# One hybrid encoder layer on one core: weight sums of the last stage in additions of 512 columns, with a new instruction order

## The chip, the cores and the metric

The kernel runs on one NeuronCore of one Trainium2 chip. The metric is device time in microseconds (us) of one execution, as a median over several. The core's engines, by the names that the profile uses, are PE (TensorE, matmuls; PEld is its weight load), DVE (VectorE), ACT (ScalarE), POOL (GpSimd) and SP (SyncE, which here only issues DMAs; SPq in the timeline). Each engine works through its own instructions in the order in which the program emits them, and waits where an operand or a room in memory is not yet there.

## The reference, cut to what matters

One layer for a prompt of 1024 tokens and a sample group of 32 tokens with 512 cached positions; the weights are shared, everything is float32.

```python
def in_proj(h, g_pre, w_in):
    u = rmsnorm(h, g_pre) @ w_in            # (.., 1024) @ (1024, 4096)
    qa, ka, va, ga, qb, kb, vb, gb = jnp.split(u, SPLIT_IDX, axis=-1)   # 8 x 512
...
def band_attention(q, k, v, q_pos, k_pos, bias_table):   # 8 heads of 64, chunks of 64
    s = jnp.einsum('bqhd,bkhd->bhqk', q, k) * ATTN_SCALE + bias_table[:, rel][None]
    ok = (k_pos >= 0) & (kc <= qc) & (kc >= qc - N_PREV_CHUNKS)
    w = jax.nn.softmax(jnp.where(ok, s, NEG_INF), axis=-1)
    return jnp.einsum('bhqk,bkhd->bqhd', w, v)

def stick_breaking(q, k, v, q_pos, k_pos):               # 8 heads of 64
    log_beta = jax.nn.log_sigmoid(z)
    log_1m = jnp.where(causal, jax.nn.log_sigmoid(-z), 0.0)
    after = lax.cumsum(log_1m, axis=3, reverse=True) - log_1m
    w = jnp.where(causal, jnp.exp(log_beta + after), 0.0)
    return jnp.einsum('bhqk,bkhd->bqhd', w, v)
...
def finish(h, oa, ga, ob, gb, w_out, g_post, p, w_ple, w_ple_gate):
    y = jnp.concatenate([oa * jax.nn.silu(ga), ob * jax.nn.silu(gb)], axis=-1) @ w_out
    h = h + rmsnorm(y, g_post)
    return h + jax.nn.sigmoid(h @ w_ple_gate) * (p @ w_ple)
```

## The kernel before

**Precision.** A float32 product is made of three matmuls of a fast format: each operand is split into a high part (h) and a low part (l), and h·h, h·l and l·h are summed in PSUM. For a weight, a DMA brings the raw tile (`wr`), ACT casts the high part (`wh`), POOL subtracts for the low part (`wl`). For attention weights the same is called `wTh` (ACT) and `wTl` (DVE).

**Stages.** After the norm of the input, the eight projections qA, kA, vA, gA, qB, kB, vB, gB are computed for one pair of heads at a time (`mm_kA2` in the program is k of group A, pair 2). Prompt and sample go through them together, 1056 tokens as three chunks of 352 columns. The heads follow in stages 1 to 8, two in each: A0, B0, A1, B1, A2, B2, A3, B3. In a stage with heads A1, for instance, PE alternates between the scores and products of attention and the projections that the next stage needs. Stages 3, 4, 7 and 8 also hold a share of the sample's attention (tiles with s in the name: `SsB0`, `PVsA0`).

**A head.** A head has eight blocks of 128 queries. The scores (`SA`, `SB`) go through DVE, ACT and POOL as tiles `be`. Then the weights must be transposed: for the first blocks PE does that (`ptwA`, `ptwB`), for the last three of A (5, 6, 7) and blocks 4 to 6 of B the tile is stored to memory (`swapA11_7` is block 7 of head 1 of pair A1), read back by four DMAs and transposed by DVE. ACT and DVE split it, and PE multiplies it with v: `PVA`, `PVB`, once for blocks 0 to 3 and once for blocks 4 to 7.

**The weight sums.** The last stages (9 to 13) multiply by w_out ("o") and w_ple_gate ("g") with a seven-product Strassen-Winograd scheme, for which sums T1 to T4 of quarters of the weights are needed. They are made ahead of time in the attention stages: stages 1 and 2 for "o", 5 and 6 for "g". `sum_weights` (L1703) loads four blocks of 128x512 (`oB…`, `gB…`; the tag `sg` has three rooms), has POOL add or subtract four times and stores each result (`sum_dro`, `sum_drg`) for the last stage to load. Eight calls make 32 sums. Each sum is two POOL instructions of 256 columns now (L1708 to L1712).

**What sets the order.** The program does not run as written. A Recorder notes every operation with its dependencies (so all rows of the profile name line L781, in the changed kernel L772, and are told apart by tile names). `order()` (L549) then plans: a forward simulation with costs for each operation, and after it `PASSES` times a backward pass that gives each operation a due time and another forward simulation by due time. In the last one the due time of an operation is shifted by a number from two tables, `AHEAD_OF` (by engine and kind of tile) and `AHEAD_AT` (by stage, engine and kind; L28 to L97). The planner lets a POOL operation and a DVE operation that reads two operands from SBUF not run at the same time (`shared`). The rooms of tiles and PSUM banks are dealt in the planned order too. All DMAs go out from SP, in one line.

**Rooms that matter here.** Raw weights `wr` have four rooms, which tiles of the sample's attention use too: `wr_kA2` must wait for the last matmul of `PVsA0`, and `wr_vA2` for the last of `SsB0`; so do the weights of gA0 for `PVsA1`.

Of the kernel before, what the change touches and what calls it, by code (L numbers as in the profile page):

```python
# [28 lines left out]
    ('ACT', ''): -307, ('ACT', 'L'): -414, ('ACT', 'Qfs'): -110, ('ACT', 'Qhs'): -859,  # L29
    ('ACT', 'S'): -381, ('ACT', 'be'): 32, ('ACT', 'g'): 244, ('ACT', 'gT'): -473,  # L30
    ('ACT', 'hnh'): 1092, ('ACT', 'kd'): 363, ('ACT', 'newh'): -483, ('ACT', 'o'): -50,
    ('ACT', 'om'): -5, ('ACT', 'p'): -1128, ('ACT', 'sq'): 108, ('ACT', 'stk'): 127,
    ('ACT', 'stq'): -682, ('ACT', 'wh'): -79, ('ACT', 'whS'): -249, ('ACT', 'xS'): -955,
    ('ACT', 'xb'): -149, ('ACT', 'yb'): -199, ('DVE', ''): -1363, ('DVE', 'Kl'): 290,
# [7 lines left out]
    ('PE', 'ptxs'): 7, ('POOL', 'be'): 315, ('POOL', 'bias'): 960, ('POOL', 'g'): 573,  # L42
    ('POOL', 'ksS'): 1098, ('POOL', 'om'): -712, ('POOL', 'r'): -536, ('POOL', 'sgg'): 1213,
# [5 lines left out]
}  # L49
AHEAD_AT = {  # L50
    (0, 'ACT', 'hnh'): -902, (0, 'ACT', 'pleo'): 783, (0, 'ACT', 'sq'): 26, (0, 'ACT', 'v'): -215,
    (0, 'PE', 'mm'): -297, (0, 'PE', 'ple'): 252, (0, 'POOL', 'wl'): -634, (0, 'SP', 'wpr'): 528,
    (0, 'SP', 'wr'): -232, (0, 'SP', 'x'): -74, (1, 'ACT', 'ot'): -442, (1, 'ACT', 'wTh'): 589,
    (1, 'ACT', 'wh'): 43, (1, 'DVE', 'S'): 928, (1, 'DVE', 'om'): 258, (1, 'DVE', 'wTl'): 279,
    (1, 'PE', 'S'): -86, (1, 'SP', 'sum'): -1097, (2, 'ACT', 'L'): 674, (2, 'ACT', 'be'): -112,
    (2, 'ACT', 'ot'): -548, (2, 'ACT', 'vt'): 555, (2, 'ACT', 'wTh'): 152, (2, 'DVE', 'om'): 60,
    (2, 'DVE', 'vt'): 389, (2, 'PE', 'S'): 43, (2, 'SP', 'o'): 677, (2, 'SP', 'sum'): 621,
    (3, 'ACT', 'Qfs'): 130, (3, 'ACT', 'stq'): 1238, (3, 'ACT', 'wh'): 323, (3, 'DVE', 'L'): -248,
    (3, 'DVE', 'Vh'): 390, (3, 'DVE', 'Vl'): 233, (3, 'DVE', 'diags'): 564, (3, 'DVE', 'om'): 40,
    (3, 'DVE', 'ot'): 169, (3, 'DVE', 'over'): 620, (3, 'DVE', 'vt'): 997, (3, 'DVE', 'vx'): 1005,  # L60
# [3 lines left out]
    (4, 'ACT', 'stq'): 92, (4, 'ACT', 'wTh'): -49, (4, 'DVE', 'Kl'): 168, (4, 'DVE', 'S'): 37,  # L64
    (4, 'DVE', 'Vl'): 530, (4, 'DVE', 'newl'): -393, (4, 'DVE', 'om'): -78, (4, 'DVE', 'v'): 323,
# [3 lines left out]
    (5, 'ACT', 'stv'): 620, (5, 'ACT', 'wTh'): 828, (5, 'ACT', 'wh'): 111, (5, 'DVE', 'S'): 706,  # L69
# [13 lines left out]
    (8, 'ACT', 'om'): -708, (8, 'ACT', 'ot'): -106, (8, 'ACT', 'sgg'): -442, (8, 'ACT', 'wTh'): 312,  # L83
    (8, 'DVE', 'Kcs'): -163, (8, 'DVE', 'Kl'): 236, (8, 'DVE', 'S'): 304, (8, 'DVE', 'Vl'): 1322,
# [702 lines left out]
def stream_step(  # L787
# [7 lines left out]
    nc = rec  # L795
# [1481 lines left out]
```

## Time and profile before

| | us |
|---|---|
| three executions | 766.77, 769.12, 770.49 (median 769.12) |
| the profiled execution | 767.52 |
| its span, first to last instruction | 765.7 |
| PE busy in the span | 755.8 |
| granted clock of PE | 1.000 of full speed |

The span is what the profile shows; the execution's own time is 1.8 us longer. The profile's rows read as follows: in the timeline, start and duration in us, engine, line, operation, the tile written and the tiles read (numbers at the end of names left out), their shapes and how many instructions the row joins; in brackets the idle time of the engine before it and what ended it. In the waits, total idle time, number of times and the longest. In the stretches, for PE, PEld, DVE, ACT and POOL in this order the busy time, with the number of instructions in brackets.

### The profile page before, as it was taken

How to read it: one execution, taken by the hardware profiler on the slowest of the kernel's cores; microseconds unless marked ns; L12 is line 12 of the kernel's file. 1: busy time of each engine (PE TensorE's matmuls, PEld its weight loads, DVE VectorE, ACT ScalarE, POOL GpSimd, SP SyncE). 2: the span in 40 equal slices, each digit the busy share in tenths (PEclk: the TensorE clock that was granted, in tenths of full speed). 3: DMA queues.
4: the chain of work that ended last, by engine and by line, in shares of the span. 5: the costliest groups of instructions: out<-in, count | busy, mean ns of one | idle time of the engine just before them, and what ended most of it. 6: DMA issues, size and time to landing. Idle time of an engine off the chain costs nothing.

```text
span 765.7 us, 14211 instructions
## 1 busy us (share of the span) xinstructions
PE 755.8 (99%) x4410; PEld 699.5 (91%) x4410; DVE 615.7 (80%) x1067; ACT 525.1 (69%) x1122; POOL 447.7 (58%) x503
## 2 busy tenths in 40 slices
PE   9999999999999999999999999999999999999997
PEld 7999999999998999999999999999998877888786
DVE  7837878898879999989798898887455688988985
ACT  6647767787766768876977786764337877784561
POOL 5623626953257555566772566778552449698453
PEclk9999999999999999999999999999999999999999
DMA  8748888778878849988878889995798856868846
GB/s 305 238 132 208 240 192 261 211 198 232 218 194 233 226 119 241 257 247 254 228 195 250 219 215 229 247 271 159 240 288 271 264 185 203 325 180 256 296 144 204
DMA packets 202525, 173.73 MB, mean 227 GB/s; under 512 B 67009, under 2 KB 164649, under 8 KB 202450
## 3 DMA queue, kind: packets, MB, share of 16 engines
q1 hardware_dynamic: 202450, 172.83, 78.7%
q8 instruction: 35, 0.57, 0.3%
q14 instruction: 40, 0.33, 0.1%
HBM read 105.72 MB, written 58.91 MB: 215 GB/s over the span
## 4 chain that ended last, share of the span: by engine, by line
PE 86%; DMA 5%; DVE 3%; ACT 2%; issue 1%; SPq 1%; POOL 0%; ACTq 0%; DVEq 0%; POOLq 0%
PE mm_vA L781 6%; PE mm_kB L781 6%; PE mm_qA L781 6%; PE mm_gA L781 6%; PE mm_gB L781 6%; PE mm_kA L781 6%; PE mm_qB L781 5%; PE PVB L781 4%; PE SA L781 3%; PE ple L781 3%; PE SB L781 3%; PE PVA L781 3%; PE o3P L781 3%; PE o1P L781 3%; PE g1P L781 3%; PE g0P L781 3%
## 5 line engine op out<-in xcount | busy, mean ns | idle before, releaser
L781 POOL TENSOR_TENSOR be<-be 128x256 f32<-128x256 f32 (+8 forms) x66 | 84.7, 1290 | 47.6 <-ACT be L781 17.8
L781 DVE TENSOR_TENSOR_SCAN be<-be,SB 128x384 f32<-128x384 f32 (+5 forms) x96 | 91.8, 962 | 12.0 <-ACT be L781 5.6
L781 ACT ACTIVATE be<-SB 128x384 f32<-128x384 f32 (+5 forms) x192 | 85.2, 499 | 18.2 <-DVE be L781 9.1
L781 DVE TENSOR_TENSOR wTl<-be,wTh 128x640 fp32r<-128x640 f32 (+2 forms) x48 | 58.6, 1228 | 4.5 <-ACT wTh L781 3.6
L781 DVE STREAM_TRANSPOSE be<-be 128x640 f32<-128x640 f32 (+3 forms) x56 | 47.7, 865 | 5.4 <-DMA be<-in_cache_b_k_dram 2.7
L781 ACT ACTIVATE be<-be,statA 128x640 f32<-128x640 f32 (+3 forms) x64 | 44.4, 695 | 10.2 <-DVE statA L781 10.0
L781 ACT CAST wTh<-be 128x640 fp32r<-128x640 f32 (+2 forms) x48 | 37.5, 785 | 4.3 <-DMA be<-swapB 2.9
L781 POOL TENSOR_TENSOR gB<-gB,gB 128x256 f32<-128x256 f32 x32 | 26.4, 845 | 18.5 <-DMA gB<-in_w_ple_gate_dram 18.5
L781 POOL TENSOR_TENSOR oB<-oB,oB 128x256 f32<-128x256 f32 x32 | 26.3, 837 | 12.7 <-DMA oB<-in_w_out_dram 10.7
L781 PE MATMUL SB<-kdB,LB 128*128 128x384 f32 (+5 forms) x96 | 33.0, 348 | 0.0
L781 PE MATMUL SB<-klB,LB 128*128 128x384 f32 (+5 forms) x96 | 33.0, 345 | 0.0
L781 DVE CUSTOM_DVE_ANT_0 be<-SA,biasA 128x320 f32<-128x320 f32 (+2 forms) x64 | 29.4, 481 | 4.0 <-PE SA L781 3.1
L781 PE MATMUL SA<-kdA,LA 128*128 128x320 f32 (+2 forms) x96 | 30.5, 322 | 0.0
L781 PE MATMUL SA<-klA,LA 128*128 128x320 f32 (+2 forms) x96 | 30.1, 317 | 0.0
L781 ACT CAST wTh<-ptwB 128x512 fp32r<-128x512 f32 (+3 forms) x48 | 22.4, 485 | 10.2 <-PE PVB L781 5.6
L781 DVE TENSOR_TENSOR wTl<-ptwB,wTh 128x512 fp32r<-128x512 f32 (+3 forms) x48 | 25.2, 543 | 3.8 <-ACT wTh L781 3.6
L781 PE MATMUL ptwB<-ident,be 128*128 128x128 f32 x144 | 26.7, 273 | 1.1 <-DVE be L781 0.7
L781 POOL TENSOR_TENSOR klA<-stkA,kdA 64x1024 fp32r<-64x1024 f32 (+2 forms) x9 | 19.9, 2215 | 10.9 <-ACT kdA L781 10.8
L781 DVE TENSOR_TENSOR LA<-stqA,LA 64x1024 fp32r<-64x1024 f32 (+2 forms) x9 | 16.7, 1857 | 10.4 <-ACT LA L781 10.2
L781 DVE TENSOR_TENSOR wTl<-ptwA,wTh 128x128 fp32r<-128x128 f32 (+3 forms) x48 | 22.1, 480 | 3.6 <-ACT wTh L781 3.4
L781 POOL TENSOR_TENSOR h<-h,x 128x512 f32<-128x512 f32 (+1 forms) x18 | 23.4, 1320 | 1.3 <-DVE h L781 1.3
L781 PE MATMUL PVB<-wTh,v2B 128*128 128x512 f32 (+1 forms) x96 | 24.1, 344 | 0.0
(694 smaller groups left out, 2652.3 us busy)
## 6 DMA issues: line engine op xcount, KB each, us to landing
swapA<-be SPq DMA_DIRECT2D x24, 320.0 KB, 3.8
be<-swapA SPq DMA_DIRECT2D x96, 80.0 KB, 2.5
oB<-in_w_out_dram SPq DMA_DIRECT2D x16, 256.0 KB, 4.5
sum_dro<-oB SPq DMA_DIRECT2D x16, 256.0 KB, 3.2
gB<-in_w_ple_gate_dram SPq DMA_DIRECT2D x16, 256.0 KB, 4.3
sum_drg<-gB SPq DMA_DIRECT2D x16, 256.0 KB, 3.3
x<-in_x_prompt_dram SPq DMA_DIRECT2D x16, 256.0 KB, 4.5
h_dr<-h SPq DMA_DIRECT2D x8, 512.0 KB, 4.5
```

The source lines that it names most:

```text
L781: getattr(getattr(tc.nc, o.what[0]), o.what[1])(*args, **kw)
```

## The change

The loop over two slices in `sub` becomes one instruction; the planner runs 2 passes in place of 9; and both tables of shifts are other tables altogether.

```diff
 AHEAD_OF = {
-    ('ACT', ''): -307, ('ACT', 'L'): -414, ('ACT', 'Qfs'): -110, ('ACT', 'Qhs'): -859,
...
+    ('ACT', 'Kh'): 207, ('ACT', 'L'): -556, ('ACT', 'be'): 73, ('ACT', 'g'): 1388,
...
 BANKS = {'mm': 1, 'S': 2, 'T': 1, 'PV': 1}
-PASSES = 9
+PASSES = 2
 PE_LATEST = True
...
         def sub(out, x, y, op):
             rec.low = 1
-            for c in (slice(0, 256), slice(256, 512)):
-                nc.gpsimd.tensor_tensor(out[:, c], x[:, c], y[:, c], op)
+            nc.gpsimd.tensor_tensor(out, x, y, op)
             rec.low = 0
```

PE, ACT, DVE and SP have the same operations as before, in another order (4410, 1021, 1067 and 918 recorded operations); POOL has 471 in place of 503.

Three places show what moved. The first is SP's queue at the weights of kA2, where heads A1 end and B1 begin (`wr_kA` raw weights, `be<-in_cache_b_k_dram` reads of the sample's cache, `o_dr<-diagsA` small stores, `be<-swapA` reads of a score tile for its transposition). Before:

```order
L781 DMA oB_2904<-in_w_out_dram 128x512
L781 DMA be<-in_cache_b_k_dram 32x16x32 x3
L781 DMA wr_kA_0_3032<-in_w_in_dram 128x4x128
L781 DMA be<-in_cache_b_k_dram 32x16x32
L781 DMA wr_kA_1_3033<-in_w_in_dram 128x4x128
L781 DMA wr_qA_0_3035<-in_w_in_dram 128x4x128
L781 DMA o_dr_63<-diagsA_2919 32x2x32 x2
L781 DMA o_dr_64<-diagsA_2919 32x2x32 x2
L781 DMA be<-swapA_7_133 32x4x160 x4
L781 DMA be<-in_cache_b_k_dram 32x16x32
L781 DMA wr_qA_1_3036<-in_w_in_dram 128x4x128
```

With the change:

```order
L772 DMA be<-swapA_7_133 32x4x160
L772 DMA wr_kA_0_3002<-in_w_in_dram 128x4x128
L772 DMA wr_kA_1_3003<-in_w_in_dram 128x4x128
L772 DMA o_dr_63<-diagsA_2854 32x2x32 x2
L772 DMA o_dr_64<-diagsA_2854 32x2x32 x2
L772 DMA be<-swapA_7_133 32x4x160 x3
L772 DMA o_dr_64<-otA_0_0_3024 64x256
L772 DMA o_dr_64<-otA_0_1_3045 64x256
L772 DMA wr_qA_0_3009<-in_w_in_dram 128x4x128
L772 DMA wr_qA_1_3010<-in_w_in_dram 128x4x128
L772 DMA be<-in_cache_b_k_dram 32x16x32 x8
```

The cache reads, four of which stood among the weights, and the load of a w_out block now follow behind them all.

The second is SP's queue at the weights of vA2, in the stage of heads B1 (`sum_dro<-oB` stores a weight sum, `vnsB` is the sample's v). Before:

```order
L781 DMA ks_drA<-ktA_3258 128x32
L781 DMA sum_dro<-oB_3358 128x512
L781 DMA vnsB_3557<-vs_drB 32x4x32
L781 DMA wr_vA_0_3565<-in_w_in_dram 128x4x128
L781 DMA vnsB_3557<-vs_drB 32x4x32
L781 DMA wr_vA_1_3580<-in_w_in_dram 128x4x128
```

With the change:

```order
L772 DMA vnsB_3502<-vs_drB 32x4x32 x2
L772 DMA wr_vA_0_3524<-in_w_in_dram 128x4x128
L772 DMA wr_vA_1_3545<-in_w_in_dram 128x4x128
L772 DMA o_dr_68<-otB_1_0_3554 64x256
L772 DMA o_dr_68<-otB_1_1_3559 64x256
```

The store of a sum has left the place ahead of the weights, and their two halves stand together.

The third is POOL at head B20, where it makes products over the score tiles (`be<-be`) block by block, wider from block to block, and weight sums between them. Before:

```order
L781 TENSOR_TENSOR be<-be 128x128
L781 TENSOR_TENSOR gB_4478<-gB_4478,gB_4469 128x256
L781 TENSOR_TENSOR be<-be 128x256
L781 TENSOR_TENSOR be<-be 128x384
L781 TENSOR_TENSOR be<-be 128x512
L781 MEMSET be 128x1
L781 TENSOR_TENSOR gB_4478<-gB_4478,gB_4469 128x256
L781 TENSOR_TENSOR gB_4469<-gB_4469,gB_4487 128x256
L781 TENSOR_TENSOR be<-be 128x640
```

With the change:

```order
L772 TENSOR_TENSOR be<-be 128x128
L772 TENSOR_TENSOR gB_4467<-gB_4467,gB_4417 128x512
L772 TENSOR_TENSOR be<-be 128x256
L772 TENSOR_TENSOR be<-be 128x384
L772 TENSOR_TENSOR be<-be 128x512
L772 MEMSET be 128x1
L772 TENSOR_TENSOR be<-be 128x640
L772 TENSOR_TENSOR be<-be 128x768
```

The first sum is whole ahead of the 256-column product, and the second pair of halves, which stood ahead of the 640-column product, is gone from there; the other sums follow later. In SP's queue at head A31 the store of a sum (`sum_drg<-gB`) moves from behind the reads of blocks 6 and 7 to ahead of them, and the cache reads from among them to behind.

More of the change, by code (lines that the diff above doesn't have):

```diff
@@ L28 @@
 AHEAD_OF = {
-    ('ACT', ''): -307, ('ACT', 'L'): -414, ('ACT', 'Qfs'): -110, ('ACT', 'Qhs'): -859,
[L30 to L34, printed above, removed]
@@ new lines @@
+    ('ACT', 'junk'): -1269, ('ACT', 'kd'): -317, ('ACT', 'newh'): 105, ('ACT', 'oT'): 655,
+    ('ACT', 'oj'): 829, ('ACT', 'ot'): 82, ('ACT', 'p'): -600, ('ACT', 'sg'): -246,
+    ('ACT', 'sq'): 1488, ('ACT', 'stk'): 373, ('ACT', 'stv'): 281, ('ACT', 'v'): 135,
+    ('ACT', 'vt'): -245, ('ACT', 'wTh'): -31, ('ACT', 'wh'): 193, ('ACT', 'whS'): -371,
+    ('ACT', 'whs'): -848, ('ACT', 'x'): 202, ('ACT', 'xS'): 146, ('DVE', 'Kcs'): -377,
+    ('DVE', 'S'): -118, ('DVE', 'Vh'): -1234, ('DVE', 'cc'): 663, ('DVE', 'diags'): -443,
@@ new lines @@
+    ('DVE', 'gj'): -557, ('DVE', 'h'): -248, ('DVE', 'lg'): -1145, ('DVE', 'lo'): 399,
+    ('DVE', 'newl'): -1399, ('DVE', 'o'): 417, ('DVE', 'ot'): -206, ('DVE', 'over'): 261,
+    ('DVE', 'sgg'): 69, ('DVE', 'sq'): -1331, ('DVE', 'ug'): -293, ('DVE', 'vx'): -746,
+    ('DVE', 'w'): -563, ('DVE', 'wl'): 252, ('DVE', 'wlS'): -338, ('DVE', 'wph'): 67,
+    ('PE', 'PVs'): -129, ('PE', 'Ss'): 57, ('PE', 'g'): -716, ('PE', 'mm'): -8,
+    ('PE', 'ptws'): 69, ('PE', 'ptx'): -592, ('PE', 'ptxs'): 19, ('POOL', 'be'): -148,
@@ L49 @@
+    ('POOL', 'gT'): -366, ('POOL', 'ogg'): 1173, ('POOL', 'om'): -1329, ('POOL', 'r'): 738,
[4 rows of a table added]
 }
 AHEAD_AT = {
[L51 to L60, printed above, removed]
[3 rows of a table removed]
@@ L77 @@
-    (7, 'ACT', 'be'): 447, (7, 'ACT', 'kd'): -699, (7, 'ACT', 'om'): -1093, (7, 'ACT', 'stv'): -159,
-    (7, 'ACT', 'wTh'): 220, (7, 'ACT', 'wh'): 657, (7, 'DVE', 'stats'): 251, (7, 'DVE', 'wTl'): 52,
[4 rows of a table removed]
-    (8, 'ACT', 'om'): -708, (8, 'ACT', 'ot'): -106, (8, 'ACT', 'sgg'): -442, (8, 'ACT', 'wTh'): 312,
-    (8, 'DVE', 'Kcs'): -163, (8, 'DVE', 'Kl'): 236, (8, 'DVE', 'S'): 304, (8, 'DVE', 'Vl'): 1322,
[3 rows of a table removed]
-    (8, 'SP', 'wr'): 210, (9, 'ACT', ''): 132, (9, 'ACT', 'ple'): -857, (9, 'ACT', 'x'): 1236,
@@ L94 @@
-    (12, 'DVE', 'gT'): -1415, (12, 'DVE', 'gj'): 887, (12, 'POOL', 's'): -859, (12, 'SP', 'hh'): 748,
-    (13, 'ACT', 'x'): -379, (13, 'DVE', 'S'): 55, (13, 'DVE', 'cc'): 684, (13, 'DVE', 'wlS'): -69,
-    (13, 'PE', 'g'): 217,
[8 rows of a table added]
+    (3, 'ACT', 'ot'): 1383, (3, 'ACT', 'wTh'): 390, (3, 'DVE', 'Kcs'): -277, (3, 'DVE', 'S'): -375,
[4 rows of a table added]
+    (4, 'ACT', 'wh'): -103, (4, 'DVE', 'Kcs'): 472, (4, 'DVE', 'Kl'): -521, (4, 'DVE', 'L'): 116,
[5 rows of a table added]
+    (5, 'SP', 'sum'): 271, (6, 'ACT', 'ot'): -780, (6, 'ACT', 'stk'): -369, (6, 'ACT', 'vt'): 573,
@@ new lines @@
+    (6, 'DVE', 'L'): -1245, (6, 'DVE', 'S'): 128, (6, 'DVE', 'om'): 182, (6, 'DVE', 'wTl'): 63,
+    (6, 'PE', 'S'): -511, (6, 'PE', 'ptw'): -7, (6, 'POOL', 'qsS'): 986, (6, 'SP', 'kd'): -122,
+    (6, 'SP', 'o'): 1350, (6, 'SP', 'to kt'): 1023, (6, 'SP', 'wr'): -186, (7, 'ACT', 'Qfs'): 251,
+    (7, 'ACT', 'om'): 873, (7, 'ACT', 'ot'): 583, (7, 'ACT', 'stk'): -453, (7, 'ACT', 'stq'): 285,
+    (7, 'ACT', 'stv'): 1422, (7, 'ACT', 'v'): -1056, (7, 'ACT', 'wTh'): 266, (7, 'ACT', 'wh'): 545,
+    (7, 'DVE', 'S'): 751, (7, 'DVE', 'Vl'): 1389, (7, 'DVE', 'over'): 168, (7, 'DVE', 'vx'): 965,
[3 rows of a table added]
@@ L97 @@
+    (8, 'ACT', 'ot'): 331, (8, 'ACT', 'whs'): -717, (8, 'DVE', 'Kl'): -964, (8, 'DVE', 'S'): -1078,
+    (8, 'DVE', 'Vl'): -1077, (8, 'DVE', 'om'): -20, (8, 'DVE', 'sgg'): 82, (8, 'DVE', 'wTl'): 746,
+    (8, 'PE', 'PV'): -346, (8, 'PE', 'S'): 114, (8, 'PE', 'Ss'): -1130, (8, 'PE', 'mm'): -282,
+    (8, 'PE', 'ptw'): -106, (8, 'PE', 'ptws'): -121, (8, 'POOL', 'ogg'): -272, (8, 'POOL', 'wl'): 364,
[6 rows of a table added]
 }
```

17 lines of the change are left out of this document (removed), and 55 rows, old and new, of tables (AHEAD_AT, AHEAD_OF).

## The prediction, on record before the changed kernel ran

> **What bounds the kernel now.** I read the page's head and its chain first, then the waits of TensorE, then busy time in stretches of 20 us, and last the timeline around each wait. The clock needs no further view: the page shows it at full speed in all forty slices.
>
> ```profile
> span 765.7 us, 14211 instructions
> PE 755.8 (99%) x4410; PEld 699.5 (91%) x4410; DVE 615.7 (80%) x1067; ACT 525.1 (69%) x1122; POOL 447.7 (58%) x503
> PE 86%; DMA 5%; DVE 3%; ACT 2%; issue 1%; SPq 1%; POOL 0%; ACTq 0%; DVEq 0%; POOLq 0%
> ...
> 760.00:765.80 5.80, 0.69 (x6) 0.48 (x5) 2.36 (x6) 0.78 (x2) 1.82 (x2) 0.95 0.38 136
> ```
>
> TensorE (PE) is busy 99% of the span and carries 86% of the chain; the changed order has the same 4410 matmuls of the same shapes. So the change can only touch 765.7 − 755.8 = 9.9 us. Of these the last 5.74 us of the span hold 0.69 us of PE work (first number after the stretch's length): 5.05 us of tail, whose instructions stand in the same order after the change. The rest is in the list of PE's waits (total, times, longest):
>
> ```profile
> PE idle L781 <- DVE newh L781: 1.3, 1, 1.3
> PE PVA L781 <- ACT wTh L781: 1.0, 1, 1.0
> PE mm_vA L781 <- ACT wh_vA L781: 0.9, 1, 0.9
> PE ptwB L781 <- DVE be L781: 0.7, 2, 0.5
> PE mm_kA L781 <- ACT wh_kA L781: 0.5, 1, 0.5
> PE ptwB L781 <- ACT be L781: 0.3, 1, 0.3
> ```
>
> The first is the start, which the new order leaves as it is. The others are 3.4 us in six stalls, and the whole question is which of these six a new order removes and which it makes.
>
> **The additions themselves.** They are 64 of 256 columns now; by form, GpSimd (POOL) shows them (those of w_out, oB, differ by 1%) and one addition of 512 columns of the same type elsewhere:
>
> ```profile
> L781 POOL TENSOR_TENSOR gB<-gB,gB 128x256 f32<-128x256 f32 x32 | 26.4, 845 | 18.5 <-DMA gB<-in_w_ple_gate_dram 18.5
> L781 POOL TENSOR_TENSOR h<-h,x 128x512 f32<-128x512 f32 x16 | 20.4, 1295 | 1.3 <-DVE h L781 1.3
> ```
>
> 64 × 0.84 = 53.8 us becomes 32 × 1.295 = 41.4 us, so POOL's busy time falls by 12 us at most. On the end I cost it at 0: POOL is busy 58% and has 0% of the chain, the PE work of the same stages hides it, and no matmul reads a sum before the last stage. Without that cover it would be worth the 12 us. What can be worth something is where the sums and everything else now stand.
>
> **The end of heads A1: the weights of kA2.**
>
> ```profile
> 210.00 0.36 PE L781 MATMUL SA<-klA,LA 128*128 128x320 f32 x1
> 220.14 0.54 SPq L781 DMA_DIRECT2D swapA<-be  x1
> 220.98 0.28 PE L781 MATMUL PVsA<-newh,newl 128*128 128x256 f32 x1
> 224.03 0.43 SPq L781 DMA_DIRECT2D wr_kA<-in_w_in_dram  x1
> 224.51 2.16 SPq L781 DMA_DIRECT2D be<-in_cache_b_k_dram  x1
> 226.72 0.49 SPq L781 DMA_DIRECT2D wr_kA<-in_w_in_dram  x1
> 229.94 2.34 SPq L781 DMA_DIRECT2D be<-swapA  x4
> 229.67 0.37 PE L781 MATMUL SB<-klB,LB 128*128 128x448 f32 x1
> 229.90 0.62 ACT L781 CAST wh_kA<-wr_kA 128x512 fp32r<-128x512 f32 x1 [3.17 <-DMA wr_kA<-in_w_in_dram]
> 230.57 0.92 PE L781 MATMUL mm_kA<-hnh,wh_kA 128*128 128x352 f32 x4 [0.54 <-ACT wh_kA L781]
> 234.15 1.45 PE L781 MATMUL mm_kA<-hnl,wh_kA 128*128 128x352 f32 x8
> 235.44 0.48 PE L781 MATMUL mm_kA<-hnh,wh_kA 128*128 128x352 f32 x2
> 236.93 0.79 PE L781 MATMUL PVA<-wTh,v2A 128*128 128x512 f32 x3 [1.01 <-ACT wTh L781]
> ```
>
> The raw weights take the room of sample tiles that PVsA's last matmul frees at 221.26 (220.98 + 0.28). SP's queue then issues a bias tile, a w_out block and three cache reads first, so that wr_kA goes out 2.77 us later, at 224.03, and its second half, behind one more cache read that held SP for 2.16 us, at 226.72. ACT idles 3.17 us for them, and PE 0.54 us.
>
> The changed queue (rows in the part on the change) has none of these between: both halves can go out as soon as the room is free, and all eight cache reads follow later. PE has 57 matmuls between PVsA's last and the first of mm_kA in both orders. The first cast gains 2.8 us, the second some 4.9 (226.72 − 221.26, less one issue of 0.5). A 0.54 us stall cannot survive that; I take it as gone, from bounds of all of it and nothing (where SP comes late to the row ahead, the reads of swapA11_7; but that tile's S matmuls stand earlier before PVsA than they did).
>
> The PVA stall is the other end of the same queue: swapA was stored at 220.14 and read back only at 229.94, behind weights and diagonals. Now one of the four reads precedes the weights and three follow the diagonals. The earlier start of all weights and the missing cache reads bring the last read to about 226; with the 2.3 us of issue the operands are there some 3 us earlier, against 1.7 us by which PVA itself comes earlier (13.5 to 11.8 us after PVsA, counted in matmuls). Gone too, with 1.3 us to spare; bounds: all and nothing.
>
> Idle time understates a stall, because ends of matmuls are modelled. From start to start: 8 matmuls of 352 columns go by in 235.44 − 234.15 = 1.29 us, 0.161 each, other widths in proportion. At mm_kA 230.57 − (229.67 + 0.20) = 0.70; at PVA 236.93 − (235.44 + 0.32) = 1.17.
>
> **Heads B1: the weights of vA2.**
>
> ```profile
> 263.76 0.41 SPq L781 DMA_DIRECT2D sum_dro<-oB  x1
> 264.37 0.29 PE L781 MATMUL SsB<-Kh1sB,QlsB 128*128 128x272 f32 x1
> 268.30 0.33 PE L781 MATMUL SB<-klB,LB 128*128 128x384 f32 x1
> 269.53 0.59 PE L781 MATMUL mm_vA<-hnh,wh_vA 128*128 128x352 f32 x2 [0.90 <-ACT wh_vA L781]
> ```
>
> The same pattern: SsB's last matmul frees the room at 264.66, PE has 20 matmuls of cover, and the weights come through 0.90 us late; start to start 269.53 − (268.30 + 0.17) = 1.06. The change puts 27 matmuls there, some of 512 columns (over 7 × 0.161 = 1.1 us more), and takes the store of a sum out from ahead. Gone; bounds all and 0.
>
> **The B heads.**
>
> ```profile
> 114.20 0.41 PE L781 MATMUL ptwB<-ident,be 128*128 128x128 f32 x2 [0.53 <-DVE be L781]
> 342.07 1.37 PE L781 MATMUL mm_vB<-hnh,wl_vB 128*128 128x352 f32 x7
> 343.64 0.52 PE L781 MATMUL ptwB<-ident,be 128*128 128x128 f32 x3 [0.20 <-DVE be L781]
> 344.51 0.33 PE L781 MATMUL mm_vB<-hnl,wh_vB 128*128 128x352 f32 x1
> 345.10 0.63 PE L781 MATMUL ptwB<-ident,be 128*128 128x128 f32 x4 [0.27 <-ACT be L781]
> ```
>
> At 343 to 345 (head B20) two transpositions wait for a weight product that POOL makes between four halves of gB. Start to start they cost 343.64 − (342.07 + 7 × 0.161) = 0.44 and 345.10 − (344.51 + 0.16) = 0.43. In the new order one addition of 512 stands ahead of the first product (1.295 for 0.84, half a microsecond later) and none of the others before the fifth, and PE's cover grows (first four blocks: 46, 54, 50, 53 matmuls between scores and transposition before; 50, 53, 60, 77 now). I take both as gone. At 114.20 (head B00) it is the other way: 43 matmuls were 0.53 us too few, and now 38 stand there: 5 × 0.161 = 0.8 us more stall. Bounds for the head: 0, since its softmax chain is reordered as well, and 2.0, if the second to fourth blocks (60, 70 and 63 matmuls to 42, 49 and 51) come short too. I take 0.8, the place's own row.
>
> **Sum.** −(0.70 + 1.17 + 1.06 + 0.44 + 0.43) = −3.8; +0.8 at B00; +0.3 for shorter covers elsewhere (heads A21 and A31, third rival; 0 to 6.8, taken near 0 as those chains have slack by the rows). Net −2.7 us. The profiled execution took 767.5 us, 1.8 of it around the span, so 764.8 us. [...] 764.8 is 0.56% under the median.
>
> **The rivals.** *All stalls in the middle go.* That takes B00's too, 0.53 us and some 0.7 with the restart, so 767.5 − 3.8 − 0.7 = 763.0. For it: an order can do this, since nothing but waiting lies in these 3.4 us. Against it: B00's shorter cover.
>
> *Nothing comes of it: the stalls are dealt anew.* Six stalls of the same size elsewhere, with B00's 0.8, give 768.3. For it: the rows of every stage moved, and the order before left six. Against it: I found no such place as clear as the five that go.
>
> *A longer hold of GpSimd's addition delays VectorE.*
>
> ```profile
> 225.73 0.81 DVE L781 TENSOR_TENSOR wTl<-be,wTh 128x640 fp32r<-128x640 f32 x1
> 235.82 1.54 POOL L781 TENSOR_TENSOR be<-be 128x768 f32<-128x768 f32 x1 [1.40 <-ACT be L781]
> 236.66 1.39 DVE L781 TENSOR_TENSOR wTl<-be,wTh 128x640 fp32r<-128x640 f32 x1
> ...
> L781 DVE TENSOR_TENSOR wTl<-be,wTh 128x640 fp32r<-128x640 f32 (+2 forms) x48 | 58.6, 1228 | 4.5 <-ACT wTh L781 3.6
> ```
>
> The same VectorE instruction takes 0.81 us alone and 1.39 where a POOL addition was running when it began, and it ends 0.69 us after that addition: it waited. [...] By the rows, an addition now holds for 1.295 us where a half held 0.845. [...] Against it: half as many additions are there to be met, VectorE is busy 80%, and only the PVA row shows wTl on PE's path today.
>
> *SP's queue makes read-back and weights late in other stages: slower.* PVA needs the last score tile through a store, a read, a transposition and a cast. In A11 that took 236.93 − 210.00 = 26.9 us.
>
> ```profile
> swapA<-be SPq DMA_DIRECT2D x24, 320.0 KB, 3.8
> be<-swapA SPq DMA_DIRECT2D x96, 80.0 KB, 2.5
> ```
>
> The store landed 3.8 us after 220.14, and the reads stood 6.0 us more in the queue. Without that the chain is 10.1 to the store, 3.8, 2.5 and some 1.9 for transposition, cast and remainder: 18.3 us. The new order cuts the cover from 181 to 136 matmuls in A21 (28.0 to 20.9 us) and from 205 to 151 in A31 (30.5 to 22.3). It decides when the reads go out over 2.6 us late in A21 or 4.0 in A31. With A11's 6.0 us of lateness the loss is 3.4 and 2.0, and at gA0, where the cover of the weights falls from 9.8 to 7.9 us against the 9.3 that kA2 took (230.57 − 221.26), 1.4: 767.5 + 6.8 = 774.3. For it: a store of a sum now stands ahead of A31's reads. Against it: fewer cache reads stand ahead of them.
>
> **Chances.** Forecast 36%, from 762.5 to 767.5; all gone 10%; dealt anew 7%; longer holds 12%; late queue 35%. About 0.5% is what a measurement of this kernel can tell from no change, so the lines are at 765.3 and 773.0. Faster: 27 of the forecast's 36 and the 10, 37%. Slower: 7 of the 12 and 31 of the 35, 38%. Within: the rest, 9 + 7 + 5 + 4, 25%. The range over all cases is 762 to 778: its upper end holds the late queue with B00's bound of 2.0 and a little of the holds.
>
> **What would show it.** Right: no wait of mm_kA, mm_vA or PVA on ACT at heads A1 and B1, ACT's idle time before wh_kA near 0, ptwB of B00 waiting 1.3 us. Wrong at the queue: PVA of A21 or A31 waiting for wTh, or mm_gA for wh_gA. Wrong at the hold: wTl<-be with a mean above the 1.2 us it has, and PE waiting for wTl. Wrong in the sum: PE's busy time not 755.8, or a tail longer than 5.05 us.

## The result, and the profile after

| | before | with the change |
|---|---|---|
| median of six executions, us | 767.92 | 773.73 |
| lowest to highest, us | 765.07 to 770.49 | 772.70 to 775.24 |
| the profiled execution, us | 767.52 | 775.24 |
| its span, us | 765.7 | 773.5 |
| mean granted clock of PE in it | 1.000 | 0.996 |

The changed kernel takes 1.0078 times as long (interval 1.0052 to 1.0104): slower by 0.8%. The prediction said 764.8 us, faster. The profiled execution is the slowest of the six, 1.5 us above the median, and the terms below are those of that execution. Its clock is among the lowest too: the six show 0.996 to 1.000, and the one at 1.000 took 772.70 us, so the lowered clock is not what most of the loss comes from.

The page's head of the changed kernel, and below it all waits of PE (total, times, longest):

```profile
span 773.5 us, 14224 instructions
PE 758.3 (98%) x4410; PEld 700.0 (91%) x4410; DVE 619.6 (80%) x1067; ACT 526.5 (68%) x1122; POOL 444.0 (57%) x471
```

```profile
PE SA L772 <- DVE statA L772: 2.3, 1, 2.3
PE idle L772 <- DVE newh L772: 1.3, 1, 1.3
PE SB L772 <- ACT be L772: 1.3, 1, 1.3
PE PVA L772 <- ACT wTh L772: 1.1, 1, 1.1
PE ptwB L772 <- DMA be<-swapB: 0.8, 1, 0.8
PE PVB L772 <- DVE v2B L772: 0.8, 1, 0.8
PE SB L772 <- DMA klB<-klB: 0.6, 1, 0.6
PE ptwB L772 <- DVE over L772: 0.5, 1, 0.5
PE mm_vB L772 <- ACT be L772: 0.4, 1, 0.4
PE mm_gA L772 <- ACT wh_gA L772: 0.4, 1, 0.4
PE ptwB L772 <- DVE be L772: 0.2, 1, 0.2
PE mm_qA L772 <- ACT be L772: 0.2, 1, 0.2
```

The span of the profiled execution grew by 7.8 us, 2 us more than the medians did. PE's idle time went from 765.7 − 755.8 = 9.9 to 773.5 − 758.3 = 15.2 us, which is 5.3 of it; PE's busy time rose by 2.5 us with the same 4410 matmuls, which is the rest. Without the start (the second row) the list holds 8.6 us where it held 3.4. The waits that were to go are gone: no mm_kA, no mm_vA, no ptwB at head B20, and the one PVA row is at another head. New ones stand in their place, that of mm_vB (at 344.97 us) at the very place of B20. Three make more than half of it, and stretches of 20 us show where they are (busy PE, PEld, DVE, ACT, POOL, then the granted clock as a share of full speed):

```profile
220.00:240.00 20.00, 18.71 (x117) 17.84 (x116) 17.97 (x30) 15.41 (x37) 10.95 (x12) 1.00 0.76 199
320.00:340.00 20.00, 17.69 (x102) 17.04 (x103) 15.91 (x34) 14.71 (x27) 9.23 (x10) 0.91 0.84 256
440.00:460.00 20.00, 18.94 (x124) 18.24 (x123) 14.94 (x27) 13.92 (x26) 9.61 (x11) 1.00 0.80 230
```

**First place, head A21 (320 us).** The timelines of PE, DVE and SP in the changed kernel, with the idle time of the engine in brackets:

```profile
322.55 0.42 PE L772 MATMUL SA<-kdA,LA 128*128 128x320 f32 x1 [2.31 <-DVE statA L772]
323.73 1.67 PE L772 MATMUL mm_qB<-hnh,wh_qB 128*128 128x352 f32 x5
...
322.00 0.49 DVE L772 CUSTOM_DVE_ANT_0 be<-SA,biasA 128x320 f32<-128x320 f32 x1 [2.88 <-DMA swapA<-be]
...
313.83 0.74 SPq L772 DMA_DIRECT2D biasA<-r_dr  x1
314.67 0.47 SPq L772 DMA_DIRECT2D klB<-klB  x1
315.18 1.47 SPq L772 DMA_DIRECT2D be<-swapA  x2
316.76 0.49 SPq L772 DMA_DIRECT2D swapA<-be  x1
317.29 4.25 SPq L772 DMA_DIRECT2D be<-swapA  x6
```

Read it backwards. PE's scores wait for statA on DVE, but DVE itself had been idle for 2.88 us: it wants to write a new score tile of A21, and the room for it is that of the last tile of head A20, which comes free when the store of that tile (swapA20_7) has landed. The store went out at 316.76, behind a bias, a klB and two reads in SP's queue, and DVE went on 5.2 us after that. So a store that nobody reads soon held PE, through a room.

The idle time is not all. Stretches of 2 us of the same kernel, same columns:

```profile
322.00:324.00 2.00, 1.45 (x6) 1.30 (x7) 1.90 (x6) 1.40 (x3) 0.00 (x0) 0.83 0.72 227
324.00:326.00 2.00, 2.00 (x8) 2.00 (x8) 1.82 (x6) 1.87 (x6) 0.14 (x2) 0.50 0.59 151
326.00:328.00 2.00, 2.00 (x13) 1.99 (x12) 1.85 (x7) 0.67 (x2) 0.00 (x0) 0.82 0.61 140
328.00:330.00 2.00, 2.00 (x16) 2.00 (x15) 1.86 (x6) 1.85 (x3) 0.79 (x2) 1.00 1.04 332
```

After the wait the granted clock is 0.50, and PE gets through 8 matmuls in 2 us where it does 16 at the full clock. Five matmuls of 352 columns take (325.20 − 323.73)/5 = 0.29 us each (the next score matmul starts at 325.20), against 0.161. By the granted clock of the first three rows, 0.34 + 1.00 + 0.36 = 1.7 us are lost behind a wait of 2.3 us. That is most of the 2.5 us by which PE's busy time grew; the rest is not the clock's, for PE's busy time is 756.4 us, 0.6 more than before, in the profile of experiment 2, which has this order and a clock of 1.00 throughout.

**Second place, head B10 (229 us).** PE, then DVE, POOL and ACT:

```profile
228.96 0.44 PE L772 MATMUL SB<-kdB,LB 128*128 128x384 f32 x1 [1.29 <-ACT be L772]
...
225.77 1.93 DVE L772 TENSOR_TENSOR wTl<-be,wTh 128x640 fp32r<-128x640 f32 x1
227.63 0.81 DVE L772 TENSOR_TENSOR_SCAN be<-be,SB 128x320 f32<-128x320 f32 x1
...
225.73 1.30 POOL L772 TENSOR_TENSOR wl_kA<-wr_kA,wh_kA 128x512 fp32r<-128x512 f32 x1
...
228.47 0.44 ACT L772 ACTIVATE be<-SB 128x320 f32<-128x320 f32 x1 [2.14 <-DVE be L772]
```

This is the place where kA2's weights were to come early, and they do: POOL makes their low part from 225.73, where before ACT only cast their high part at 229.90. But the low part now starts 0.04 us ahead of a wTl of DVE, which takes 1.93 us where it takes 0.81 alone, and which ends 0.67 us after the low part (227.70 and 227.03), as the wTl at 236.66 in the kernel before ended 0.69 us after a product of POOL; the scan, the activation and PE's scores stand behind it. What DVE waits for here is the low part of a weight, not a weight sum.

**Third place, head A30 (443 us).** PE, then SP:

```profile
443.49 0.85 PE L772 MATMUL PVA<-wTh,v2A 128*128 128x512 f32 x4 [1.06 <-ACT wTh L772]
...
426.46 0.53 SPq L772 DMA_DIRECT2D swapA<-be  x1
...
428.31 5.93 SPq L772 DMA_DIRECT2D out_dram<-ktB  x4
...
436.92 2.92 SPq L772 DMA_DIRECT2D be<-swapA  x4
```

The last score tile of A30 is stored at 426.46 and read back only at 436.92. The four stores of ktB ahead of the read hold SP for 5.93 us. Before, at A11, a read-back was late in the same way, behind weights, cache reads and small stores (stored at 220.14, read from 229.94).

**The additions.** POOL's groups by form:

```profile
L772 POOL TENSOR_TENSOR gB<-gB,gB 128x512 f32<-128x512 f32 x16 | 23.3, 1459 | 9.9 <-DMA gB<-in_w_ple_gate_dram 8.2 <-DMA out_dram<-vtA 1.4
L772 POOL TENSOR_TENSOR oB<-oB,oB 128x512 f32<-128x512 f32 x16 | 21.6, 1348 | 20.0 <-DMA oB<-in_w_out_dram 13.1 <-PE SA L772 6.7
```

32 additions take 44.9 us in place of the 41.4 worked out, and POOL's busy time fell by 3.7 us, not 12. The rows of the additions alone fell by 7.8 us (26.4 + 26.3 before); POOL's other work takes 4.1 us more.

### The profile page after: what moved, and what is told of

It reads as the page before. It is cut to its first block, busy times and chain, and to the rows that moved or that the text cites. A ratio compares the mean times of both kernels' runs of the same rounds, so it can differ in the third digit from the quotient of the medians.

```text
span 773.5 us, 14224 instructions
## 1 busy us (share of the span) xinstructions
PE 758.3 (98%) x4410; PEld 700.0 (91%) x4410; DVE 619.6 (80%) x1067; ACT 526.5 (68%) x1122; POOL 444.0 (57%) x471
## 4 chain that ended last, share of the span: by engine, by line
PE 75%; DMA 9%; SPq 5%; ACT 3%; issue 3%; DVE 3%; POOL 2%; ACTq 0%; DVEq 0%; POOLq 0%
PE mm_kB L772 6%; PE mm_vA L772 6%; PE mm_qA L772 6%; PE mm_gB L772 5%; PE mm_kA L772 5%; SPq L772 5%; PE mm_qB L772 4%; PE PVB L772 4%; PE SA L772 3%; PE ple L772 3%; PE o3P L772 3%; PE g1P L772 3%; PE o1P L772 3%; PE g0P L772 3%; PE o2P L772 2%
## 5 line engine op out<-in xcount | busy, mean ns | idle before, releaser
L772 POOL TENSOR_TENSOR be<-be 128x512 f32<-128x512 f32 (+8 forms) x66 | 85.8, 1305 | 57.9 <-DVE be L772 21.7
L772 DVE TENSOR_TENSOR wTl<-be,wTh 128x640 fp32r<-128x640 f32 (+2 forms) x48 | 55.3, 1162 | 7.1 <-ACT wTh L772 6.8
L772 DVE CUSTOM_DVE_ANT_0 be<-SA,biasA 128x320 f32<-128x320 f32 (+4 forms) x64 | 29.9, 481 | 7.0 <-PE SA L772 3.3
L772 PE MATMUL SA<-kdA,LA 128*128 128x320 f32 (+3 forms) x96 | 31.1, 326 | 2.3 <-DVE statA L772 2.3
L772 POOL TENSOR_TENSOR oB<-oB,oB 128x512 f32<-128x512 f32 x16 | 21.6, 1348 | 20.0 <-DMA oB<-in_w_out_dram 13.1
L772 PE MATMUL SA<-klA,LA 128*128 128x320 f32 (+3 forms) x96 | 30.8, 323 | 0.0
L772 POOL TENSOR_TENSOR gB<-gB,gB 128x512 f32<-128x512 f32 x16 | 23.3, 1459 | 9.9 <-DMA gB<-in_w_ple_gate_dram 8.2
L772 PE MATMUL ptwB<-ident,be 128*128 128x128 f32 x144 | 26.3, 273 | 1.6 <-DMA be<-swapB 0.8
L772 POOL TENSOR_TENSOR sggB<-sggB,oggB 128x352 f32<-128x352 f32 x12 | 14.9, 1239 | 15.2 <-DVE sggB L772 10.9
L772 PE MATMUL PVA<-wTh,v2A 128*128 128x512 f32 (+3 forms) x96 | 22.6, 319 | 1.1 <-ACT wTh L772 1.1
L772 PE MATMUL PVA<-wTl,v2A 128*128 128x512 f32 (+1 forms) x96 | 23.2, 325 | 0.0
```

The costliest lines, as they stand in the source:

```text
L772: getattr(getattr(tc.nc, o.what[0]), o.what[1])(*args, **kw)
```

## The experiments

Two theories stood at the start. **Order**: the time comes from the new order alone; single places can be named and mended. **Hold**: it comes from the longer additions, which hold DVE (in the kernel before, a wTl of 640 columns that began at 165.14 us, inside a half of oB, took 1.24 us where it takes 0.81 alone, and ended 0.69 us after that half). In the edits below, `later(x, y)` puts x right behind y in the planned list of operations, on one engine's queue, and everything else keeps its place; names are those of the program. Ratios are to the kernel before on the same chip, with a 95% interval; its medians there were 767.0 to 767.8 us.

### 1. The old order with whole additions

The order is planned with pairs of halves, as before; then the first of each pair is left out, and the second is issued with all 512 columns.

```diff
...
+                if o in self.first:
+                    continue
+                o.args = self.second.get(o, o.args)
...
```

> The order of before, instruction for instruction on every engine; only each pair of 256-column additions becomes one of 512 at the place of the second. Theory 'order': the loss of 5.8 us (773.7 to 767.9) comes from the new order alone, so this runs as before, 767.9 within 1.5 us, and its stalls of PE are the six of before. Theory 'hold' (a longer hold of GpSimd's additions delays VectorE): most of the loss is here, 771 to 774, and VectorE's wTl<-be is longer than its mean of 1228 ns.

767.40 us, 1.0004 (0.9987 to 1.0020). One addition of 512 in place of two of 256, with nothing else moved, is worth nothing either way. (Its waits are not quite the six of before: mm_kA's is absent, and ptwB waits once, 0.99 us at 492 us, for a product of POOL, with no weight sum near it. So single waits of this size differ between executions of nearly the same program.)

### 2. The new order with halved additions

The other way round: each addition of the changed kernel's plan is issued as two halves, one right behind the other.

```diff
...
+                if o in self.whole:
+                    for c in (slice(0, 256), slice(256, 512)):
+                        getattr(getattr(tc.nc, o.what[0]), o.what[1])(*[x[:, c].get() for x in o.args[:3]], o.args[3])
+                    continue
...
```

> The new order, instruction for instruction, but each 512-column addition is made in two halves of 256, one right behind the other. Theory 'order': 773.7 within 1.5 us, with the new waits (scores waiting for statA at 320 us, SB for be at 227 us, PVA for wTh at 442 us) still there. Theory 'hold': 768 to 770.

772.62 us, 1.0083 (1.0050 to 1.0115): the whole loss is there without a single long addition. The mean of DVE's wTl says the same in the four kernels: 1228 ns before, 1245 in the old order with whole additions, 1162 with the change, 1188 in the new order with halves. It goes with the order and is lower in the slower ones. Hold falls. In this kernel's profile the wait of SB for be at B10 is 0.18 us, the wait at A21 is 0.42 us and the clock 1.00; only PVA's at A30 (1.12 us) has its size, so two of the three waits expected there all but went, while the time of the order stays. That profile is of the quickest of six executions (770.41 us); three others at a clock of 1.000 took 772.1 to 774.3 us. At A21 the store went out at 314.52, 2.2 us earlier than with the change, while DVE came to this point at the same time, so that it waited 1.00 us there and not 2.88.

### 3 and 4. What the planner does with other tables

The old tables and 9 passes with the new additions, and the new tables with 9 passes:

```diff
-            for c in (slice(0, 256), slice(256, 512)):
-                nc.gpsimd.tensor_tensor(out[:, c], x[:, c], y[:, c], op)
+            nc.gpsimd.tensor_tensor(out, x, y, op)
```

> Before, with only the two additions of 256 written as one of 512; planner, its 9 passes and its two tables as before, so the order is planned anew from the old tables. Theory 'tables fit one program': the shifts were right for one list of operations, and with another the planner deals the waits anew: 771 to 780, PE waits of over 1 us in places where before has none. Rival: the shifts are general, 767.9 within 1.5 us.

```diff
-PASSES = 2
+PASSES = 9
```

> The new kernel with the planner's 9 passes of before in place of 2; tables and additions are the new ones. Theory 'tables fit one plan': the new shifts belong to the plan after two passes, and on another plan they are noise: 775 to 790, slower than the new order. Rival: two passes are too few, and nine give a better order: 765 to 771.

777.82 us, 1.0143 (1.0102 to 1.0184), and 790.81 us, 1.0294 (1.0256 to 1.0331). With 32 operations fewer, the old tables give an order that by the medians is slower than that of the new tables (the two intervals overlap by a hair), and nine passes make the new tables slower still. That tables fit one plan only is the reading at hand; two cases don't prove it. The first of the two has one long wait of PE, and the clock falls behind it (PE's timeline, then a stretch of 5 us):

```profile
449.13 1.41 PE L781 MATMUL PVA<-wTh,v2A 128*128 128x512 f32 x4 [4.15 <-DVE wTl L781]
```

```profile
450.00:455.00 5.00, 5.00 (x19) 5.00 (x19) 4.97 (x11) 3.55 (x7) 4.97 (x6) 0.50 1.01 275
```

### 5 and 6. The store at A21, earlier and later

In the changed kernel, the store of swapA20_7 is put ahead of four DMAs, or behind the six reads that follow it:

```diff
+        store = find("SP", "swapA20_7")
+        for x in (find("SP", "beA20_5", "swapA20_5", n=1), find("SP", "beA20_5", "swapA20_5", n=0), find("SP", "klB20"), find("SP", "biasA30")):
+            later(x, store)
```

> The new order, but on SP's queue the store of score tile swapA20_7 goes ahead of a bias load, a key load and two read-backs that stood before it. Theory 'room': the 2.3 us wait of the A21 scores is for the room of that tile, which the store leaves only when it has landed; the store goes out some 3 us sooner (near 313.8, not 316.8), the wait falls to under 0.3 us and with it the stretch of reduced clock behind it (0.91 in 320:340), so 768.5 to 771. Rival 'tile late': the tile itself is late, because VectorE's v2A<-vtA took 3.11 us beside GpSimd at 309 us; then the store cannot go sooner and the time stays within 1 us of 773.7.

```diff
+        later(find("SP", "swapA20_7"), find("SP", "beA20_6", "swapA20_6", n=3))
```

> The new order with the suspected cost doubled: the store of swapA20_7 goes behind six read-backs, some 4 us later than in the new order. Theory 'room': the wait of the A21 scores grows from 2.3 to about 6 us, and TensorE's granted clock is 0.5 for some 4 us behind it, in every execution; 776 to 780. Rival: the room is not what the scores wait for; 773.7 within 1.5 us.

Earlier: 771.65 us, just above what was expected, 1.0058 (1.0036 to 1.0080). Later: 776.15 us, 1.0123 (1.0099 to 1.0147). The unchanged order lies between them. SP's and PE's rows, first of the earlier store, then of the later one:

```profile
314.12 0.32 SPq L785 DMA_DIRECT2D swapA<-be  x1
...
320.18 0.31 PE L785 MATMUL SA<-kdA,LA 128*128 128x320 f32 x1
```

```profile
319.28 0.60 SPq L784 DMA_DIRECT2D swapA<-be  x1
...
323.77 0.64 PE L784 MATMUL SA<-kdA,LA 128*128 128x320 f32 x1 [3.71 <-DVE statA L784]
```

With the store 2.6 us earlier the scores don't wait; with it 2.5 us later they wait 3.71 us in place of 2.31 (about 6 were expected, of a store some 4 us later). The stretches of the later store show the clock behind it, which stays down for longer than after 2.31 us (at 0.50 some 6.8 us by these rows, 3.4 there):

```profile
322.00:326.00 4.00, 2.23 (x8) 2.23 (x9) 2.65 (x7) 1.95 (x5) 0.14 (x2) 0.54 0.64 177
326.00:330.00 4.00, 4.00 (x19) 3.99 (x17) 3.71 (x13) 1.65 (x4) 0.00 (x0) 0.61 0.81 242
```

So the room is the cause at this place. The gain of the earlier store alone, some 1.5 us by the ratios, is not told apart from nothing by its interval; the loss of the later one is, against the earlier.

### 7 to 9. The other two places, and all three together

In the changed kernel: DVE's wTl of A11 goes behind the scan of B10; the four stores of ktB go behind the read-back of A30; and a third kernel does both and the earlier store.

```diff
+        later(find("DVE", "wTlA11_1", "beA11_6"), find("DVE", "omB10_4", "omB10_4", "SB10_4_1"))
```

> The new order, but on VectorE the wTl of A11's block 6 goes behind the scan of B10's block 4. Theory 'collision': SB's wait of 1.3 us at 227 is that wTl (two SBUF operands) waiting for GpSimd's wl_kA and holding the scan back; with the scan ahead the wait is under 0.3 us. Rival: the scan's own operands are late (ACT's be at 226.1); then about 1 us stays.

```diff
+        read = find("SP", "beA30_7", "swapA30_7", n=3)
+        for n in (3, 2, 1, 0):
+            later(find("SP", "out_4_dram", "ktB3", n=n), read)
```

> The new order, but the four stores of ktB3 on SP's queue go behind the read-back of swapA30_7 instead of ahead of it. Theory 'late queue': PVA's wait of 1.1 us at 442 is the read-back standing 6.6 us (436.9 less 426.5 + 3.8) behind these stores; the reads go out 3 to 5 us sooner and the wait is gone. Rival: wr_vB3, which stays ahead, or ACT's cast of it is what comes last there; then the wait stays within 0.3 us.

> The new order with all three moves: the store of swapA20_7 ahead, the stores of ktB3 behind the read-back, the scan ahead of wTl. If the three waits are what the new order lost and nothing new takes their place, some 2.3 + 2.5 (clock) + 1.1 + 1.3 us less than the profiled 775.2 and 3 to 4 less than the median: 769 to 771. If waits are dealt anew each time, 771 to 773.

One execution each: 773.06 us for the scan, 771.54 us for the stores, which tells nothing by time; in each profile the wait in question is gone and the other two are still there, though that at A21 is 0.88 and 0.39 us in place of 2.31. All three, in six executions: 770.48 us, 1.0040 (1.0026 to 1.0053). All three waits are gone; by the medians that returns about half of the loss (0.4 of 0.8%), and the intervals of this and of the change only just touch. What stays is eleven waits of 0.2 to 0.8 us; the largest are ptwB for swapB (0.8) and for over (0.7), and they were not traced further.

### 10 to 14. Is a removed stall a gain at all?

The prediction counted −3.8 us for stalls that go. They went in the changed kernel, but so much else moved that their worth can't be read there. So they were taken out of the old order, one after the other, at heads A1 and B1.

First the weights of kA2 alone, ahead of the block of w_out and the cache reads:

```diff
+        last = find("SP", "wr_kA2_1")
+        for x in [find("SP", "KcsB0", "in_cache_b_k_dram", n=n) for n in (3, 2, 1, 0)] + [find("SP", "oB223")]:
+            later(x, last)
```

> The order of before, but on SP's queue both halves of wr_kA2 go ahead of the w_out block and the four cache reads, as the new order has it. Theory 'term': the prediction priced this place rightly; wr_kA2 goes out as PVsA's last matmul ends (2.8 us sooner), the waits of mm_kA (0.5) and PVA (1.0) go, 765.3 to 766.5 (ratio 0.9975 to 0.999). Rival 'collision': weights that come sooner make GpSimd's wl_kA start sooner, beside VectorE's wTl and the stick-breaking scans, and a wait of SB or ptwB of about 1 us takes the place, as in the new order at 227 us; 767 within 1 us.

768.66 us, 1.0010 (0.9995 to 1.0025). The wait for wh_kA is gone, and one for wl_kA stands there (POOL, then PE):

```profile
229.76 1.44 POOL L794 TENSOR_TENSOR oB<-oB,oB 128x256 f32<-128x256 f32 x2 [2.97 <-DMA oB<-in_w_out_dram]
231.16 2.53 POOL L794 TENSOR_TENSOR wl_kA<-wr_kA,wh_kA 128x512 fp32r<-128x512 f32 x2
...
232.48 0.75 PE L794 MATMUL mm_kA<-hnh,wl_kA 128*128 128x352 f32 x3 [1.38 <-POOL wl_kA L794]
```

POOL idles for the block of w_out that now comes later, and the weights' low part stands behind it. A DMA that is moved back must be followed on every engine that has its reader ahead of what the move was for.

Then DVE's transposition of the cached keys, behind two scans, since DVE had idled 2.36 us for it ahead of PVA's chain:

```diff
+        later(find("DVE", "KcsB0", "KcsB0"), find("DVE", "omB10_5", "omB10_5", "SB10_5_0"))
```

> The order of before with one instruction moved on VectorE: the transposition of the sample's cached keys (be 128x512, at 230.46, after 2.36 us of waiting for the cache reads) goes behind the two scans of B10's block 5. Theory 'held engine': PVA's wait of 1.0 us at 237 is not the late read-back of swapA that the prediction named, but VectorE standing at this transposition until the cache reads land, with scans and ACT behind it; the wait falls to under 0.3 us, time 766 to 767.5 (ratio 0.997 to 1.0). Rival 'read-back': the read-back goes out as late as before (229.9), so PVA's wait stays 0.7 to 1.1 us.

767.19 us, 1.0004 (0.9990 to 1.0018); PVA's wait stays at 1.05 us, ACT idling for the weights. Both together, with the additions of that block behind wl_kA2 on POOL:

```diff
+        for n in (1, 0):
+            later(find("POOL", "oB223", "oB223", "oB123", n=n), find("POOL", "wl_kA2_1"))
```

> The order of before with everything at the end of heads A1 moved as it must: wr_kA2 ahead of the cache reads (as in weights_first), the additions of oB223 behind wl_kA2 on GpSimd, the cached keys' transposition behind the scans on VectorE. Theory 'queues behind the moved load': weights_first lost its gain because GpSimd stood at an addition whose load had been pushed back (wait of mm_kA for wl_kA, 1.4) and VectorE at the transposition; with both moved no wait of over 0.3 us is left from 220 to 240 us, and the time is 765 to 766.5 (ratio 0.996 to 0.999). Rival: waits are dealt anew in the next place; 767 to 768.5.

767.78 us, 1.0018 (1.0000 to 1.0037). mm_kA waits no more; PVA waits 1.44 us, and now the chain ends at the read-back (ACT's cast for it):

```profile
235.53 0.72 ACT L797 CAST wTh<-be 128x640 fp32r<-128x640 f32 x1 [1.24 <-DMA be<-swapA]
```

So this wait had three holders one behind the other: ACT at wh_kA, DVE at the cached keys, and the read-back in SP's queue. With the read-back ahead of cache reads and diagonals as well:

```diff
+        read = find("SP", "beA11_7", "swapA11_7", n=3)
+        keys = [find("SP", "KcsB0", "in_cache_b_k_dram", n=n) for n in range(4)]
+        for x in keys[::-1] + [find("SP", "wr_qA2_0")]:
+            later(x, read)
+        for x in [find("SP", d, "diagsA0", n=n) for d in ("o_dr1", "o_dr0") for n in (1, 0)]:
+            later(x, keys[3])
```

> whole_place with one more queue put right: on SP the four read-backs of swapA11_7 and wr_qA2's first half go ahead of the cache reads and the diagonals. Theory 'one queue at a time': in whole_place the last thing that PVA waited for (1.4 us) was the read-back itself, out at 231.9; it now goes out near 224 to 226, no wait over 0.3 us is left between 220 and 240 us, and the 1.9 us that the prediction priced there are gained: 765 to 766.3 (ratio 0.997 to 0.9995). Rival 'dealt anew': what is moved back (cache reads, wr_qA2) makes a wait of 0.5 to 1.5 us before 280 us, and the time is 767 within 1 us.

768.91 us, 1.0028 (1.0009 to 1.0047). The place is clean now, and the next one is not. Stretches of 20 us, of before and then of this kernel:

```profile
220.00:240.00 20.00, 18.45 (x115) 17.36 (x115) 17.00 (x30) 12.11 (x29) 12.87 (x16) 1.00 0.91 223
240.00:260.00 20.00, 20.00 (x129) 19.66 (x128) 18.82 (x23) 13.04 (x27) 12.45 (x16) 1.00 0.82 234
```

```profile
220.00:240.00 20.00, 19.89 (x128) 19.32 (x127) 18.54 (x31) 12.82 (x30) 12.95 (x16) 1.00 0.90 205
240.00:260.00 20.00, 18.88 (x116) 17.62 (x116) 16.52 (x21) 12.21 (x24) 12.08 (x13) 1.00 0.86 248
```

PE wins 1.44 us of work and 13 matmuls in the first stretch and loses 1.12 us and 13 matmuls in the second, where its products PVA and PVB wait for DVE. The third row is POOL's:

```profile
243.50 0.79 PE L803 MATMUL PVA<-wTl,v2A 128*128 128x512 f32 x3 [0.44 <-DVE wTl L803]
249.87 0.84 PE L803 MATMUL PVB<-wTh,v2B 128*128 128x512 f32 x4 [0.54 <-DVE v2B L803]
...
242.02 4.32 POOL L803 TENSOR_TENSOR oB<-oB,oB 128x256 f32<-128x256 f32 x4 [3.33 <-DMA oB<-in_w_out_dram]
```

DVE does not lack time there (busy 16.52 us in the second stretch, 18.82 before). Ahead of v2B it stands idle for 2.40 us for a product of POOL, and that product stands behind these four additions, for which POOL idled 3.33 us (0.69 before): their block of w_out went out at 238.42, where before it went out at 237.04. So one more load in SP's queue is late; that is read from the trace, and no run moved it. The profiled execution (767.31 us) is one of the quickest of twelve; the rows explain that nothing is won, not why the median is 1.8 us above before's.

Last, the same kernel with two score matmuls as cover ahead of mm_vA2:

```diff
+        score = find("PE", "SB11_5_1", n=1)
+        for n in (1, 0):
+            later(find("PE", "mm_vA2_0", "wh_vA2_0", n=n), score)
```

> readback_too, and at vA2 two score matmuls of B11 go ahead of the first two of mm_vA on PE (0.35 us more work while the weights come). Theory 'cover': the wait of mm_vA for wh_vA falls from 1.0 to about 0.6 us and nothing else moves: 0.3 us less than readback_too, too little for the medians, to be seen in the wait alone. Rival: the scores are not ready there and PE waits for them instead.

768.37 us, 1.0010 (0.9995 to 1.0024). mm_vA's wait falls to 0.24 us (it was 0.9 before), but the scores that were pulled ahead wait 0.63 us for DVE right there, and PVB waits 1.04 us. Nothing is won. No kernel tried beats the one before.

## Why the prediction was wrong, point by point

- **The additions at nothing, POOL hidden: right.** Runs 1 and 2 show it from both sides. That POOL's busy time would fall by up to 12 us was off (3.7), since a whole addition took 1.35 to 1.46 us and not 1.295, and POOL's other work grew by 4.1 us; nothing hung on it.
- **The stalls at mm_kA, PVA of A11, mm_vA and B20 gone: right as places, but for half of B20.** None of these waits is in the list after; at B20's place mm_vB now waits 0.44 us for ACT, as it does in every profile with the new order, against the 0.87 us that was to be won there. PVA's was put down to the late read-back; runs 10 to 13 show that this was only the last of three holders.
- **Their worth, −3.8 us: not shown to be a gain.** The sum took the length of a stall as its price. Taken out of the old order, the first two gave 1.0028 (1.0009 to 1.0047), no gain: in the profile most of the time came back within 20 us as waits for DVE, behind the next load in SP's queue. mm_vA's was taken out only together with these, and B20's was not tried by itself.
- **+0.8 us at B00: too large.** With five matmuls less of cover the wait there is 0.25 us. The 0.53 from which the term was built is that of one execution: the kernels with the old order in experiments 1 and 10 to 14 show 0.23 or 0.24 at this place. So the shorter cover cost nothing that can be seen, the bound of 0 that the text named.
- **"+0.3 for shorter covers elsewhere (heads A21 and A31, third rival; 0 to 6.8, taken near 0 as those chains have slack by the rows)": this step failed.** In the profiled execution the new waits are 8.4 us (8.6 less B00's), and 1.7 us of lowered clock come with them. In the medians the three largest places, mended together, are worth some 3 of the 5.8 us. The covers that were counted held: there is no wait of PVA in A21 or A31. The same comparison was not made for A30, where the stores of ktB are now ahead of the read-back, and rooms were not looked at: which tile's room the next one takes, and what frees it. That was the largest.
- **The rivals.** "SP's queue makes read-back and weights late in other stages: slower", 774.3 us, came nearest to 773.7, with a chance of 35%. That its number is so near is luck: it is the sum of 3.4 us at A21, 2.0 at A31 and 1.4 at gA0, and of these only 0.4 us at gA0 is in the profile. Its mechanism is there at A30 (1.1 us), at gA0 and, as a store that frees a room, at A21; two of its three places were wrong. "A longer hold of GpSimd's addition" falls by runs 1 and 2, and its sign, a mean of wTl above 1.2 us, did not come (1162 ns). What such holds add up to, of which the top of the range takes in a little, no run shows; run 1 shows 1.0004 in its place. "Dealt anew" names what happened, but at twice the size: it allowed 3.4 + 0.8 us of waits, and 8.6 stand in the profile.
- **Still open:** about half of the loss, 0.4% of the time, which stays when the three places are mended. Its profile has eleven small waits, and no run tells how much each is worth. Nor can one profile: PE's first products, ple at 7 to 8 us, wait for nothing in the profile of the change and 1.31 us in that of experiment 2, whose order is the same.

## What to carry to other kernels

A change that deals the order anew can't be priced by the stalls that it removes: here 8.4 us of new waits came where 2.9 us went. Go through every store, read-back and room of every head alike, not through those near the old stalls. A stall taken out of an engine that is 99% busy need not be a gain: here the next waits took it back. So move one place in the old order and look at the next 20 us, and profile more than one execution before a wait of half a microsecond goes into a sum. And split such a change in two first (old order with the new operation, new order with the old one): two runs settled here which half it was.

## What the runs showed of the hardware that was not expected

The granted clock fell to half behind waits of PE of 2.31, 3.71 and 4.15 us (0.50 at 324 to 326 us, 0.54 at 322 to 326, 0.50 at 450 to 455), and behind shorter ones as well: 1.74 us in the kernel of the later store (0.50 at 450 to 452; a wait of 0.64 us stood 2.5 us ahead of it) and 1.78 us in the new tables with nine passes (0.52 at 322 to 324). Behind a wait of 1.73 us in the latter and one of 1.62 us in experiment 11 it stayed at 1.00, and so it did behind the waits of 1.29 and 1.06 us of the changed kernel. So between 1.6 and 1.8 us both were seen, and what decides there was not shown. In two cases the clock did not fall in the wait itself: behind 2.31 us it fell some 0.8 us after PE had started again, behind 1.74 us some 1.5 us after, and in both it stayed down for some 3.4 us. The wait of 2.31 us cost 4.0 us in all, with the 1.7 us lost behind it.

How long a store holds SP's queue is not fixed by its kind: the four of ktB at A30 took 5.93 us to issue in the changed kernel and 3.40 us where they stand behind the read (experiment 8), and single ones of the sixteen took from 0.34 to 3.17 us in the changed kernel.
